# A norm and the two projections behind it, issued in a written order, and the mixer's last weights given to two token tiles first

## The chip, the cores and the metric

The kernel runs on one core of a Trainium2 chip. The metric is the device time of one execution in microseconds (us). Three executions of the kernel before took 3191.44, 3194.19 and 3197.66 us; their median is 3194.19 us.

The core has five engines with queues of their own: TensorE (PE in the profile, with its weight loads as PEld), VectorE (DVE), ScalarE (ACT), GpSimd (POOL) and SyncE (SP, which here only issues DMAs). Each executes its own queue in order; they wait for each other through semaphores.

## What is computed

A trunk of two layers over 512 tokens of 1024 elements, all in float32. A conditioning vector gives each layer a shift, a scale and a gate for each sub-layer. In each layer:

```
h = rmsnorm(x, norm_mix) * (1 + sc1) + sh1
x = x + g1 * mixer(h)      # projections of h, a gated MLP, stick-breaking attention, an output projection
h = rmsnorm(x, norm_ffn) * (1 + sc2) + sh2
x = x + g2 * peer(h)       # q = h @ wq; scores against keys; top 16 of 256; experts' u and v rows
```

and a last `rmsnorm`. So four times in the program a norm of x stands between the product that completes x and the projections that read h.

## The kernel before, in words

The 512 tokens are four tiles of 128, and the 1024 elements eight blocks k of 128. Every large product is made of three matmuls on numbers split in a high and a low part (`mm3`, lines 125 to 128): high by high, high by low, low by high. A weight block is loaded by SP's queue into `raw` (two buffers); ScalarE copies its high part into `hi`, and VectorE subtracts to get `lo` (`split`, lines 110 to 115; `weights`, lines 117 to 123). `hi` and `lo` have three buffers each, so at most three weight blocks are split at a time, and a fourth has to wait until the matmuls on the first are done. Every ninth of the PEER's query weights is subtracted on GpSimd instead (line 521).

`normed` (lines 154 to 180) makes h. It takes the tokens in two halves, tiles 2 and 3 first. GpSimd multiplies each tile's x by its reciprocal root mean square (line 166). Then, for each of four chunks of two blocks k, TensorE transposes four 128x128 pieces into PSUM (line 173), ScalarE applies scale and shift (line 176, into `tk`), and VectorE splits the result into `hh` and `hl` (lines 114 and 115). In the PEER the first half's `tk` is also transposed back (line 493), since tile 3's tokens need h with tokens on partitions (`hrow`, line 498).

Behind the norm the projections run through `ahead` (lines 130 to 136): eight blocks `w_qk` and twelve row blocks in the mixer, sixteen blocks `wq` in the PEER. Each of the first kind is 24 matmuls of 512 columns (`qk_item`, lines 274 to 283; `q_item`, lines 508 to 521), and reads h of all four tiles. The row blocks of the last group of the mixer, `vv`, are copied out of PSUM by VectorE (line 325); the attention's logits, which come next (`logits`, lines 345 to 364), use the same PSUM banks.

The mixer ends with `out_item` (lines 410 to 429): two halves of the columns, four weight blocks each, and for each block the four tiles in the order 3, 2, 0, 1. At the last block the tile's residual is added (`residual`, lines 209 to 212: two products and two sums of 128x512 for both column halves), its squares are summed on ScalarE and their root taken (`stats`, lines 148 to 152), all of which the next norm waits for. In layer 0 the modulation vectors are still being made meanwhile: `fill(n)` puts n steps into the program (`mod_steps`, lines 186 to 195), each a DMA of 512 KB and one pass of VectorE over 128x1024. The PEER ends (lines 827 to 842) with the last two weight blocks' matmuls for the tiles 2, 0 and 1 in turn, each followed by the residual and `stats`.

What sets the order: the program text gives each instruction a priority, and a scheduler at build time puts each engine's queue together, taking at every moment of its own model the earliest instruction whose inputs are ready. Under `high_priority` (lines 271 and 495) a region goes ahead of everything else. Under `manual_schedule` (line 800) the instructions of the region stay in the written order on each engine, and where they fall among the others is still the scheduler's choice. `keep_in_program_order` puts one instruction behind the one written before it on its engine: so the load of ScalarE's exponential table (line 343). Two operand-free steps of the PEER, an iota and sixteen memsets into the free part of the big array `act` (lines 551 to 554), run on GpSimd.

## Time and profile before

| | |
|---|---|
| median of three executions | 3194.19 us |
| the profiled execution's own time | 3192.75 us |
| its span | 3191.0 us |
| TensorE busy | 2993.4 us, 94% of the span |
| VectorE busy | 2505.6 us, 79% |
| ScalarE busy | 1177.2 us, 37% |
| GpSimd busy | 908.3 us, 28% |

The span is the time from the first to the last instruction on the core; the execution's time is 1.75 us more. Times in the rows are us from the start of the span, unless marked ns. A group's row gives count, busy time and mean duration of one; a bracket at the end of a timeline row gives how long the engine was idle before and what released it.

### The profile page before, as it was taken

To read this page: it belongs to the slowest core of one execution; us is meant where nothing else is said; L and a number is where in the kernel's file an instruction comes from. 1 tells how busy PE (TensorE), PEld (TensorE's weight loads), DVE (VectorE), ACT (ScalarE), POOL (GpSimd) and SP (SyncE) were. 2 spreads that over 40 slices of the span, in tenths; PEclk is the share of its full clock that TensorE was granted. 3 is DMA by queue.
4 is the path that set the end of the run, shared out by engine and by line. 5 is a ranking of instruction groups with operands and counts; after the bars stand their busy time and mean duration, and the time that the engine had idled before them with its cause. 6 is when DMAs were issued, how large, how long until landed. Compare 5 with 4: busy or idle time off the path is not lost.

```text
span 3191.0 us, 47164 instructions
## 1 busy us (share of the span) xinstructions
PE 2993.4 (94%) x17516; PEld 2633.3 (83%) x17516; DVE 2505.6 (79%) x4925; ACT 1177.2 (37%) x2016; POOL 908.3 (28%) x634
## 2 busy tenths in 40 slices
PE   6988988999999999999989989899999999999997
PEld 4776878998777999977777878889987789998776
DVE  7687799698777889777754448969887788996777
ACT  3253333333333433333333533334333334333333
POOL 1002012103555323345410010230055443333452
PEclk8989999999999999999999899999999999999999
DMA  8746223436888666688732022232388876667885
GB/s 302 251 152 212 80 73 106 133 107 240 304 302 287 246 222 234 239 322 298 276 102 86 3 99 80 93 132 100 133 297 315 303 271 230 228 240 256 308 303 203
DMA packets 178840, 651.45 MB, mean 204 GB/s; under 512 B 19850, under 2 KB 20274, under 8 KB 178610
## 3 DMA queue, kind: packets, MB, share of 16 engines
q1 hardware_dynamic: 104018, 378.14, 35.2%
q0 software_dynamic: 73728, 268.47, 22.5%
q8 instruction: 137, 2.24, 0.3%
q10 hardware_dynamic: 864, 1.84, 0.2%
q14 instruction: 93, 0.76, 0.1%
HBM read 642.08 MB, written 6.29 MB: 203 GB/s over the span
## 4 chain that ended last, share of the span: by engine, by line
PE 23%; DVE 8%; issue 7%; DMA 6%; POOL 5%; ACT 1%; POOLq 0%; DVEq 0%; ACTq 0%
PE u L126 4%; PE u L128 3%; PE u L127 3%; PE b L126 2%; PE b L128 2%; PE b L127 2%; DVE hrow L747 1%; DVE lo L115 1%; PE z L351 1%; DMA raw<-in_ut 1%; DVE act L595 1%; PE b L387 1%; PE acc L128 0%; PE acc L127 0%; PE acc L126 0%
## 5 line engine op out<-in xcount | busy, mean ns | idle before, releaser
L126 PE MATMUL u<-hh,hi 128*128 128x384 f32 x2048 | 704.6, 344 | 22.2 <-ACT act L476 19.4
L128 PE MATMUL u<-hh,lo 128*128 128x384 f32 x2048 | 690.9, 337 | 13.9 <-DVE lo L115 13.8
L127 PE MATMUL u<-hl,hi 128*128 128x384 f32 x2048 | 689.2, 337 | 0.0
L128 PE MATMUL acc<-hi,hl 128*128 128x512 f32 x1536 | 607.4, 395 | 34.6 <-DVE hl L115 34.6
L127 PE MATMUL acc<-lo,hh 128*128 128x512 f32 x1536 | 603.2, 393 | 7.1 <-DVE lo L115 6.9
L112 ACT ACTIVATE hi<-raw 128x1024 fp32r<-128x1024 f32 x368 | 388.8, 1058 | 587.7 <-PE b L127 163.1
L126 PE MATMUL acc<-hi,hh 128*128 128x512 f32 x1536 | 601.4, 392 | 0.0
L115 DVE TENSOR_TENSOR lo<-raw,hi 128x1024 fp32r<-128x1024 f32 x332 | 407.0, 1226 | 208.6 <-ACT hi L112 207.7
L126 PEld LDWEIGHTS u<-hh,hi 128*128 128x128 f32 x2048 | 387.3, 189 | 27.2 <-ACT act L476 22.3
L128 PEld LDWEIGHTS u<-hh,lo 128*128 128x128 f32 x2048 | 387.3, 189 | 17.8 <-DVE lo L115 17.7
L127 PEld LDWEIGHTS u<-hl,hi 128*128 128x128 f32 x2048 | 388.3, 190 | 0.1
L112 ACT ACTIVATE hh<-act 128x384 fp32r<-128x384 f32 x256 | 134.4, 525 | 684.4 <-PE acc L127 680.8
L128 PEld LDWEIGHTS acc<-hi,hl 128*128 128x128 f32 x1536 | 290.2, 189 | 113.5 <-DVE hl L115 54.4
L127 PEld LDWEIGHTS acc<-lo,hh 128*128 128x128 f32 x1536 | 290.1, 189 | 75.3 <-DVE lo L115 14.4
L126 PEld LDWEIGHTS acc<-hi,hh 128*128 128x128 f32 x1536 | 290.3, 189 | 58.7
L115 DVE TENSOR_TENSOR lo<-wide,hi 128x1024 fp32r<-128x1024 f32 x232 | 282.8, 1219 | 2.2 <-ACT hi L112 2.2
L112 ACT ACTIVATE hi<-wide 128x1024 fp32r<-128x1024 f32 x232 | 242.7, 1046 | 0.1
L115 POOL TENSOR_TENSOR lo<-raw,hi 128x1024 fp32r<-128x1024 f32 x36 | 93.6, 2599 | 496.4 <-ACT hi L112 478.1
L126 PE MATMUL b<-hh,hi 128*128 128x512 f32 x384 | 150.3, 395 | 20.6 <-DVE hh L114 19.2
L115 DVE TENSOR_TENSOR hl<-act,hh 128x384 fp32r<-128x384 f32 x256 | 141.2, 551 | 14.4 <-ACT hh L112 13.8
L190 DVE SCALAR_TENSOR_TENSOR aw<-aw,crow 128x1024 f32<-128x1024 f32 x96 | 119.4, 1247 | 39.6 <-DMA aw<-in_ada 39.3
L127 PE MATMUL b<-hl,hi 128*128 128x512 f32 x384 | 150.1, 392 | 0.5 <-DVE hl L115 0.5
(1505 smaller groups left out, 4995.2 us busy)
## 6 DMA issues: line engine op xcount, KB each, us to landing
raw<-in_ut SPq DMA_DIRECT2D x256, 512.0 KB
wide<-in_v_rows SPq DMA_DIRECT2D x232, 512.0 KB
aw<-in_ada SPq DMA_DIRECT2D x96, 512.0 KB
raw<-in_wq SPq DMA_DIRECT2D x32, 512.0 KB
raw<-in_w_row SPq DMA_DIRECT2D x24, 512.0 KB
raw<-in_v_rows SPq DMA_DIRECT2D x24, 512.0 KB
raw<-in_w_qk SPq DMA_DIRECT2D x16, 512.0 KB
raw<-in_w_o SPq DMA_DIRECT2D x16, 512.0 KB
```

The lines of the kernel that those rows point to most:

```text
L112: A.activation(dst_hi, src, AF.Copy)
L115: sub.tensor_tensor(dst_lo, src, dst_hi.bitcast(F32), OP.subtract)
L126: T.matmul(o, lh, rh, start=first, stop=False)
L127: T.matmul(o, lh, rl, start=False, stop=False)
L128: T.matmul(o, ll, rh, start=False, stop=last)
L190: V.scalar_tensor_tensor(aw, aw, 1.0, crow[0], op0=OP.mult, op1=OP.mult, accum_out=modc[:, l, j:j + 1])
L351: T.matmul(z[:, b], qk[rw_, 4 + p_, i * P:(i + 1) * P], qk[rw_, p_, t * P:(t + 1) * P], start=b in (0, 4), stop=False, skip_group_check=True)
L387: T.matmul(po[:, tiles.index(t)], e[:, b], vv[:, i, h * 64:(h + 1) * 64], start=i == 0, stop=i == t)
L595: V.tensor_tensor(pr[:, :w], pr[:, :w], pr[:, w:2 * w], op)
L747: V.scalar_tensor_tensor(gacc, r, wgt[:, n - P:n - P + 1], gacc, op0=OP.mult, op1=OP.add)
```

## The change

The norm is cut into functions: `scales`, `scaled` (the scaling pass, now VectorE's), `chunk` (transposes, scale and shift, split). `normed` still exists, for layer 0's first norm. The three other norms, those of both PEERs and of layer 1's mixer, are issued by `opening`, in a region whose order on each engine is as written: the first two projections' weights and accumulators are taken ahead of the norm, and their matmuls are cut in two token halves of 256 columns, so that the sums over the tiles 2 and 3 stand between the chunks of the two halves.

```
-    def normed(pool, ps, l, which, hi, lo, after=None):
+    def scaled(pool, t0):
...
+            V.tensor_scalar_mul(xn[t], held["xs"][:, t], xstat[t])
...
-                G.tensor_scalar(xn[t], held["xs"][:, t], xstat[t], 0.0, OP.mult, OP.add)
...
+    def opening(pool, ps, l, which, hi, lo, srcs, tks):
+
+        with tc.manual_schedule():
+            scs = scales(pool, l, which)
+            ws = [weights(src) for src in srcs]
+            pq = [ps.tile([P, S], F32, name="b") for _ in srcs]
+
+            def sums(t0, q):
+                ts = slice(t0 * P, (t0 + 2) * P)
+                for k in (2 * q, 2 * q + 1):
+                    sl = slice(k * P, (k + 1) * P)
+                    for (wh, wl), o in zip(ws, pq):
+                        for n, (lh, rh) in enumerate(((wh, hi), (wh, lo), (wl, hi))):
+                            T.matmul(o[:, ts], lh[:, sl], rh[:, k, ts], start=t0 == 2 and k == 0 and n == 0,
+                                     stop=t0 == 0 and k == KD - 1 and n == 2, skip_group_check=True)
+
+            xn = scaled(pool, 2)
+            for q in range(4):
+                chunk(ps, l, which, scs, xn, 2, q, hi, lo, tks(2, q))
+            xn = scaled(pool, 0)
+            for q in range(3):
+                sums(2, q)
+            chunk(ps, l, which, scs, xn, 0, 0, hi, lo, tks(0, 0))
+            sums(2, 3)
+            for q in range(1, 4):
+                chunk(ps, l, which, scs, xn, 0, q, hi, lo, tks(0, q))
+            for q in range(4):
+                sums(0, q)
+        return pq
```

In the mixer, layer 1 uses it; the copy of `vv` out of PSUM goes to ScalarE; and the last three weight blocks of `w_o` are all taken before their matmuls, which go through the tiles 3 and 2 first and then through 0 and 1:

```
+                if l == 0:
+                    with tc.high_priority():
+                        normed(nm, ps, l, 0, hh, hl)
+                    opened = []
+                else:
+                    opened = opening(nm, ps, l, 0, hh, hl, [w_qk[l, j] for j in range(OPEN)],
+                                     lambda t0, q: nm.tile([P, 2, 2 * P], F32, name="tk", bufs=2))
...
-                ahead([qk_item(j) for j in range(8)]
+                for j, pq in enumerate(opened):
+                    qk_done(j, pq)
+                ahead([qk_item(j) for j in range(len(opened), 8)]
...
-                      + row_items(w_row[l, 2], lambda t, pr: V.tensor_copy(vv[:, t], pr)))
+                      + row_items(w_row[l, 2], lambda t, pr: A.activation(vv[:, t], pr, AF.Copy)))
...
-                ahead([out_item(half, kk) for half in range(2) for kk in range(4)])
+                ahead([out_item(0, kk) for kk in range(4)] + [out_item(1, 0)])
+                ended = [out_item(1, kk)[0]() for kk in range(1, 4)]
+                for tiles in (ORDER[:2], ORDER[2:]):
+                    for kk in range(1, 4):
+                        out_item(1, kk, tiles)[1](ended[kk - 1])
                 fill(96)
```

In the PEER the scaled tokens of the first half are kept in the free part of `act`, and the transposes back come after the opening; the iota is kept behind what is written before it on GpSimd. `qk_done` and `q_done` are the ends of the old items, split off.

```
-                    with tc.high_priority():
-                        normed(nm, ps, l, 1, hh, hl, back)
-                    for half, ph in enumerate(kept):
+
+                    free = act[0][:, :12].rearrange("p b t -> p (b t)")
+                    tks = [free[:, n * 512:(n + 1) * 512].rearrange("p (a t) -> p a t", a=2) for n in range(6)]
+                    opened = opening(nm, ps, l, 1, hh, hl, [wq[l, j] for j in range(OPEN)],
+                                     lambda t0, q: tks[q] if t0 else tks[4 + q % 2])
+                    for half in range(2):
+                        ph = ps.tile([P, 512], F32, name="b")
+                        for k in range(4 * half, 4 * half + 4):
+                            T.transpose(ph[:, k % 4 * P:(k % 4 + 1) * P], tks[k // 2][:, k % 2, P:], ident)
                         A.activation(hrow[:, half * 512:(half + 1) * 512], ph, AF.Copy)
...
-                    ahead([q_item(j) for j in range(16)])
+                    for j, pq in enumerate(opened):
+                        q_done(j, pq)
+                    ahead([q_item(j) for j in range(len(opened), 16)])
...
-                    G.iota(jk, pattern=[[1, 16], [0, P]], base=0, channel_multiplier=0,
+                    first_ = G.iota(jk, pattern=[[1, 16], [0, P]], base=0, channel_multiplier=0,
                            allow_small_or_imprecise_dtypes=True)
+                    tc.keep_in_program_order(first_)
```

## Rows read from the trace of the kernel before

**Rows 1.** The page's busy times: us (share of the span) xinstructions

```profile
PE 2993.4 (94%) x17516; PEld 2633.3 (83%) x17516; DVE 2505.6 (79%) x4925; ACT 1177.2 (37%) x2016; POOL 908.3 (28%) x634
```

**Rows 2.** TensorE's timeline, three norms: start us, us, work [idle <-releaser]

```profile
298.78 0.39 PE L128 MATMUL b<-hi,hl 128*128 128x512 f32 x1
320.34 0.94 PE L126 MATMUL b<-hh,hi 128*128 128x512 f32 x3 [0.69 <-PE b L173]
...
1614.32 0.39 PE L128 MATMUL acc<-hi,hl 128*128 128x512 f32 x1
1629.61 1.02 PE L126 MATMUL b<-hh,hi 128*128 128x512 f32 x3
...
1870.21 0.39 PE L127 MATMUL b<-lo,hh 128*128 128x512 f32 x1
...
1873.16 0.39 PE L128 MATMUL b<-hi,hl 128*128 128x512 f32 x1
...
1890.57 0.94 PE L126 MATMUL b<-hh,hi 128*128 128x512 f32 x3 [0.69 <-PE b L173]
```

**Rows 3.** Timeline of TensorE, layer 0, where the attention logits begin

```profile
166.56 2.50 PE L351 MATMUL z<-qk 64*128 64x128 f32 x10 [7.49 <-DVE uvw L325]
```

**Rows 4.** Line 325, both layers: who waited for it (us, times)

```profile
  PE z L351: 8.3, 2
```

**Rows 5.** Timeline of ScalarE, a projection's result copied out of PSUM

```profile
1636.63 0.58 ACT L281 ACTIVATE qk<-b 128x512 f32<-128x512 f32 x1
```

**Rows 6.** Tile tk, durations of one in ns (min/median/max)

```profile
L176 ACT ACTIVATE tk<-b,modc,sc x64: 554/564/581, 21.5 to 1892.8; 128x256 f32<-128x256 f32 x64
L114 DVE CAST hh<-tk x48: 409/422/1220, 23.3 to 1893.4; 128x512 fp32r<-128x512 f32 x48
L115 DVE TENSOR_TENSOR hl<-tk,hh x48: 678/691/1481, 24.8 to 1893.9; 128x512 fp32r<-128x512 f32 x48
...
L212 DVE TENSOR_TENSOR xs<-xs,tk x16: 680/683/1997, 276.1 to 1875.6; 128x512 f32<-128x512 f32 x16
```

**Rows 7.** Tile xn, durations of one in ns (min/median/max)

```profile
L166 POOL TENSOR_SCALAR xn<-xs,rs x16: 1114/1394/2622, 9.8 to 1887.0; 128x1024 f32<-128x1024 f32 x16
```

**Rows 8.** The page's costliest groups: the two passes over a loaded weight block

```profile
L112 ACT ACTIVATE hi<-raw 128x1024 fp32r<-128x1024 f32 x368 | 388.8, 1058 | 587.7 <-PE b L127 163.1
...
L115 DVE TENSOR_TENSOR lo<-raw,hi 128x1024 fp32r<-128x1024 f32 x332 | 407.0, 1226 | 208.6 <-ACT hi L112 207.7
```

**Rows 9.** Timeline of VectorE, four one-input passes of 512 elements

```profile
1830.06 1.68 DVE L240 TENSOR_SCALAR y<-y,rsy 128x512 f32<-128x512 f32 x4 [1.12 <-POOL rsy L141]
```

**Rows 10.** Windows, layer 1's PEER norm: each engine's busy time, PEclk, DMA share, GB/s

```profile
1875.00:1878.00 3.00, 0.00 (x0) 0.00 (x0) 2.63 (x6) 2.77 (x5) 2.81 (x2) 0.59 1.02 416
1878.00:1882.00 4.00, 2.29 (x9) 1.60 (x10) 0.51 (x2) 1.02 (x2) 4.00 (x5) 0.50 0.84 338
1882.00:1886.00 4.00, 3.73 (x15) 2.58 (x14) 3.07 (x6) 2.60 (x6) 3.56 (x17) 0.52 0.02 6
1886.00:1890.00 4.00, 2.62 (x18) 1.96 (x18) 1.98 (x3) 2.45 (x6) 2.44 (x3) 1.00 0.00 0
```

**Rows 11.** TensorE's timeline, attention of layer 1: 256-column matmuls among others

```profile
1779.89 0.28 PE L377 MATMUL z<-sh,tri 128*128 128x256 f32 x1
1780.01 0.40 PE L376 MATMUL z<-sl,tri 128*128 128x512 f32 x1
...
1781.39 0.60 PE L373 MATMUL z<-sh,tri 128*128 128x256 f32 x3
```

**Rows 12.** Timeline of GpSimd in layer 1's PEER norm

```profile
1879.95 1.94 POOL L551 IOTA act<- 128x2048 f16 x1
```

**Rows 13.** Timeline of VectorE, a modulation step beside GpSimd's work, layer 0

```profile
295.30 3.08 DVE L190 SCALAR_TENSOR_TENSOR aw<-aw,crow 128x1024 f32<-128x1024 f32 x1 [1.16 <-DMA aw<-in_ada]
```

**Rows 14.** Timeline of TensorE, the first projection of the program

```profile
40.54 1.19 PE L126 MATMUL b<-hh,hi 128*128 128x512 f32 x2 [19.21 <-DVE hh L114]
```

**Rows 15.** VectorE's timeline, the program's start: a modulation step and its wait

```profile
18.50 1.23 DVE L190 SCALAR_TENSOR_TENSOR aw<-aw,crow 128x1024 f32<-128x1024 f32 x1 [0.96 <-DMA aw<-in_ada]
```

More of the change, by code (lines that the diff above doesn't have):

```diff
@@ L51 @@
 LOOK = 2
+OPEN = 2
 QM = 9
@@ L152, in stats, with scales @@
         rsqrt_mean(xstat[t], ss, D, 1)
-    def normed(pool, ps, l, which, hi, lo, after=None):
+    def scales(pool, l, which):
         m = modc[:, l]
@@ L160, in normed, with chunk @@
                                    col(l, which)[:, 2 * q:2 * q + 2], op0=OP.add, op1=OP.mult)
-        sh = m[:, 24 * which:24 * which + 8]
+        return scs
+    def scaled(pool, t0):
+        xn = {}
+        for t in (t0, t0 + 1):
+            xn[t] = pool.tile([P, D], F32, name="xn", bufs=2)
+            V.tensor_scalar_mul(xn[t], held["xs"][:, t], xstat[t])
+        return xn
+    def chunk(ps, l, which, scs, xn, t0, q, hi, lo, tk):
+        sh = modc[:, l, 24 * which:24 * which + 8]
+        pt = ps.tile([P, 2, 2 * P], F32, name="b")
+        for kk in range(2):
+            k = 2 * q + kk
+            for t in (t0, t0 + 1):
+                T.transpose(pt[:, kk, (t - t0) * P:(t - t0 + 1) * P], xn[t][:, k * P:(k + 1) * P], ident)
+        for kk in range(2):
+            k = 2 * q + kk
+            A.activation(tk[:, kk], pt[:, kk], AF.Identity, scale=scs[q][:, kk:kk + 1], bias=sh[:, k:k + 1])
+        both = slice(t0 * P, (t0 + 2) * P)
+        split(hi[:, 2 * q:2 * q + 2, both], lo[:, 2 * q:2 * q + 2, both], tk, V)
@@ L162, in normed @@
+    def normed(pool, ps, l, which, hi, lo):
+        scs = scales(pool, l, which)
         for t0 in (2, 0):
-            xn = {}
-            for t in (t0, t0 + 1):
-                xn[t] = pool.tile([P, D], F32, name="xn", bufs=2)
-                G.tensor_scalar(xn[t], held["xs"][:, t], xstat[t], 0.0, OP.mult, OP.add)
+            xn = scaled(pool, t0)
             for q in range(KD // 2):
-                pt = ps.tile([P, 2, 2 * P], F32, name="b")
-                tk = pool.tile([P, 2, 2 * P], F32, name="tk", bufs=2)
-                for kk in range(2):
-                    k = 2 * q + kk
-                    for t in (t0, t0 + 1):
-                        T.transpose(pt[:, kk, (t - t0) * P:(t - t0 + 1) * P], xn[t][:, k * P:(k + 1) * P], ident)
-                for kk in range(2):
-                    k = 2 * q + kk
-                    A.activation(tk[:, kk], pt[:, kk], AF.Identity, scale=scs[q][:, kk:kk + 1], bias=sh[:, k:k + 1])
-                both = slice(t0 * P, (t0 + 2) * P)
-                split(hi[:, 2 * q:2 * q + 2, both], lo[:, 2 * q:2 * q + 2, both], tk, V)
-                if after is not None and t0 == 2:
-                    after(q, tk[:, :, P:])
+                chunk(ps, l, which, scs, xn, t0, q, hi, lo, pool.tile([P, 2, 2 * P], F32, name="tk", bufs=2))
@@ L408, in mixer, with out_item @@
                 po = {}
-                def out_item(half, kk):
+                def out_item(half, kk, tiles=ORDER):
                     def use(w):
                         wh, wl = [a.rearrange("p (a b) -> p a b", a=2) for a in w]
-                        for t in ORDER:
+                        for t in tiles:
                             if kk == 0:
@@ L485, in peer @@
                 with tc.tile_pool(name="nm", bufs=1) as nm:
-                    kept = []
-                    def back(q, src):
-                        if q % 2 == 0:
-                            kept.append(ps.tile([P, 512], F32, name="b"))
-                        for kk in range(2):
-                            o = (q % 2 * 2 + kk) * P
-                            T.transpose(kept[-1][:, o:o + P], src[:, kk], ident)
-                    with tc.high_priority():
-                        normed(nm, ps, l, 1, hh, hl, back)
-                    for half, ph in enumerate(kept):
+                    free = act[0][:, :12].rearrange("p b t -> p (b t)")
[6 more added lines that the diff above has]
+                            T.transpose(ph[:, k % 4 * P:(k % 4 + 1) * P], tks[k // 2][:, k % 2, P:], ident)
                         A.activation(hrow[:, half * 512:(half + 1) * 512], ph, AF.Copy)
@@ L514, in use, with q_done @@
                             mm3(pq, wh[:, sl], wl[:, sl], hh[:, k], hl[:, k], k == 0, k == KD - 1)
-                        qts[j] = qp.tile([P, S], F32, name="qt", bufs=4)
-                        A.activation(qts[j], pq, AF.Copy)
-                        if ranked:
-                            best(*ranked.pop(0))
-                        if j % 4 == 3:
-                            ranked.extend((t, j - 3, score(t, j - 3)) for t in order)
-                    return lambda: weights(wq[l, j], G if j % QM == 1 else V), use
+                        q_done(j, pq)
+                    return lambda: weights(wq[l, j], G if j % QM == 1 else V), use
+                def q_done(j, pq):
+                    qts[j] = qp.tile([P, S], F32, name="qt", bufs=4)
+                    A.activation(qts[j], pq, AF.Copy)
+                    if ranked:
+                        best(*ranked.pop(0))
+                    if j % 4 == 3:
+                        ranked.extend((t, j - 3, score(t, j - 3)) for t in order)
                 ranked = []
```

9 lines of the change are left out of this document (6 added, 3 removed).

## The prediction

> **What bounds the kernel now.** TensorE is busy in 94% of the span [rows 1], so time can come from TensorE's work or from its roughly 190 us of idling; the change adds and removes almost no work, so I looked for the idling at the places it touches. The timeline of TensorE shows three holes in dense work, one at each norm that gets the new order. The dense work before them ends at the last row's start plus its 0.39 us, and the next projection's matmuls start at the first row with `hh` in it [rows 2]: 299.17 to 320.34 (PEER, layer 0), 1614.71 to 1629.61 (mixer, layer 1) and 1873.55 to 1890.57 (PEER, layer 1). The holes are 21.2, 14.9 and 17.0 us, 53.1 together. Only transposes run in them. A fourth hole is at the logits of layer 0, where TensorE waits 7.49 us for VectorE's copies of `vv` [rows 3].
>
> **What the openings are worth.** The unit is the dense matmul of 512 columns: between the rows at 1870.21 and 1873.16 there are 13 steps in 2.95 us, 0.227 us each [rows 2]. The first two projections, 48 matmuls, took 10.9 us behind each hole. Now they run inside it, as 96 matmuls of 256 columns. A 256-column one, with its own weight load, starts 0.12 us before the next matmul [rows 11]: 11.5 us in all, 1.44 us for each `sums` of twelve.
>
> I work out layer 1's PEER in us from E, the end of the mixer's last matmul.
> - Two tiles first: the second half of the last three blocks is 2 x 3 x 6 matmuls, 8.2 us, so tile 2 is complete at E-8.2 and tile 3 at E-9.5; by the old order it was E-2.7 and E-4.1. Their residuals (two passes of 0.68 us each [rows 6]) and roots are done well before E.
> - Weights: three blocks are split at a time, so the second projection's block can be split only when the middle one of the last three is done, E-2.7. ScalarE's pass of 1.06 and VectorE's of 1.23 [rows 8] put it at E-0.4. It is written ahead of the scaling passes, so these wait for it too. The third of the last `w_o` blocks must wait for the block before the three, E-16.3, and is ready at E-14 against a need at E-10.9; I cost that at nothing, with 3 us of cover.
> - VectorE then has residuals 0 and 1 (1.36 each, the second not before E) to E+2.3, and two scaling passes. Such a pass isn't in the trace on VectorE; bounds are 0.42 for 512 elements [rows 9] and GpSimd's 1.39 for 1024 [rows 7]. I take twice the first, 0.84, the nearest kind. E+4.0.
> - First chunk: four transposes at the low clock, 15 in 3.73 us [rows 10], 1.0; ScalarE twice 0.56, VectorE 0.42 and 0.69 [rows 6]. E+7.2; three more chunks at VectorE's 1.1 each, E+10.5. Then the second half's scaling, E+12.2; by then three `sums` are done (the third can't start before E+9.4).
> - Second half: transposes 0.6 (18 in 2.62 us at full clock [rows 10]), ScalarE 1.1, four chunks on VectorE to E+18.3, the last `sums` to E+19.8. The other `sums` lie beside this. The eight transposes back, once inside the hole, now follow: 1.2 us, E+21.0.
>
> Take off the 10.9 us that the two projections cost anyway, and the hole is 10.1 us instead of 17.0: **6.9 us** gained. In layer 0's PEER the same 10.1 stand against 21.2: **11.1**. There the old hole was longer because GpSimd had iota and memsets ahead of the second half's scaling (the same row in layer 1 [rows 12]) and VectorE had modulation steps. In layer 1's mixer the residual of the last tile is four passes, 2.7, and both final weight blocks are held to E, so the second block's split follows E too: 2.7 + 1.2 + 1.7 puts the first transposes at E+5.6 instead of E+4.0; no transposes back. 10.5 against 14.9: **4.4**.
>
> **What comes off that.** The clock: 1.3 us after E it had fallen to the lower of its levels in part, stayed at 0.50 to 0.52 (1.2 GHz) through 8 us in which only transposes ran, and was back at 1.00 (2.4 GHz) in the stretch after [rows 10]. In the new order TensorE also idles after E, so the first `sums` meet the low clock. At double spacing two of them cost 2.9 us more, of which 1.3 lie before E+12.2: 1.5 an opening, **-4.5**. Bounds are 0 and all 96 matmuls (a rival below). Layer 0's modulation steps: the last nine now stand before the tiles 3 and 2 are complete, at twice the density; a pass is 1.2 us, up to 3.08 beside GpSimd [rows 13, 15]. Bounds 0 and nine passes, 11 us; they started E-16 and end near E, so I take **-1.5**. The query block that GpSimd split goes to VectorE, before E, hidden. Layer 0's first norm has its four scaling passes on VectorE, whose splits TensorE waits for there [rows 14]: bounds +1 (no port shared with GpSimd) and -3.4; VectorE also waits for DMAs between its steps, 0.96 us in one [rows 15], so **-0.5**.
>
> **The copies of `vv`.** ScalarE does the same copy in 0.58 [rows 5], right behind each tile's last matmul: the logits can begin some 0.6 us plus a release after 159.07 instead of 7.49. **+6.3**; bounds 0 (ScalarE is late: the table load is now written behind the copies) and 6.9. What follows, the gating and the attention, keeps its own pace and moves forward. Of the 8.3 us in both layers [rows 4], 0.8 are layer 1's, where a copy of the same length still ends the wait: nothing. The iota, kept behind earlier GpSimd work, is needed only behind sixteen projections of over 5 us each: nothing.
>
> **Sum.** 6.9 + 11.1 + 4.4 - 4.5 - 1.5 - 0.5 + 6.3 = 22.2 us. The profiled execution took 3192.75 us, 1.44 under the median of 3194.19; the sum makes it 3170.6, and on the median's footing **3172 us**. Behind the openings TensorE sets the pace until the gathers, which hang on the steps and not on absolute times, so I let the gain stand to the end.
>
> **A rule against it.** The two matmuls 0.12 us apart [rows 11] show a weight load hidden behind a 256-column stream. The Trainium skill, "TensorE: Matmul & The Clock Gate", section "The mechanism", says that a weight load overlaps with a matmul in flight only if it targets another row group; here every load fills all rows. By that, with the page's 107 ns for a load and some 109 for the stream, each of the 96 would cost 0.216 us, some 9 us more an opening, and the sum would be some 5 us slower than before; the rows contradict it, and what is left of it is the first rival.
>
> **The rivals.**
> - *Loads show at 256 columns.* Three 256-column matmuls in a group took 0.60 us where one takes 0.28: 0.16 apart [rows 11]. Then 96 x 0.04 = 3.8 us an opening: 22.2 - 11.5 = 10.7, 3183.5 us. For: twelve in a row, with alternating weights. Against: the 0.12. 10%.
> - *The order holds only within the region.* Other work is put between its steps, the third projection's block above all (1.06 on ScalarE, 1.23 on VectorE [rows 8]): 2.3 us an opening, 6.9 in all, 3179 us. For: where the region's steps fall among others is the scheduler's choice. Against: both engines have pauses that could take it. In this way the change wouldn't do quite what it says. 10%.
> - *Only the copies pay.* The strict order makes VectorE a chain with waits of its own (weight splits, the squares of tile 1, modulation steps) and the openings end where the old ones did: -5.8 us, 3188. 12%.
> - *Slower: the clock stays low through the openings.* Place: from E to the last `sums`. Price: 32 transposes at 0.25 and 96 matmuls at 0.24 are 31 us. From E+4.0, with 2 us of transposes back and less the 10.9, that is 26.1 against 21.2 and 17.0; in the mixer 25.7 against 14.9: 24.8 lost, 5.8 kept by copies and start, 3213 us. It decides when some 74 of the 96 run at half rate (26.7 us over three openings, at 0.12 each). For: openings are a patchwork of short bursts. Against: the clock was back while only transposes ran, with gaps [rows 10]. 7%.
>
> **How the numbers follow.** My forecast has 61%, with a range of its own of 3158 to 3182. A measurement of this kernel can tell 0.2%, 6.4 us, from no change. Faster by more: the forecast, the first two rivals, and a little of the third, 0.83. Within: most of the third, 0.09. Slower: the clock, and a bit for a late block in the mixer, 0.08. The range that holds eight of ten reaches from 3156 (no clock loss, no modulation loss, shorter scaling) to the third rival, 3188.
>
> **What would show it.** TensorE's timeline: the hole before the first `sums` about 7 us in the PEERs and 8.5 in the mixer, matmuls of 256 columns 0.12 us apart, the last `sums` some 20 us after E; logits of layer 0 at about 160. VectorE the busiest engine from E to the last chunk. I am wrong if the 256-column steps are 0.16 or more, if the granted clock stays at 0.5 past the third `sums`, if E itself comes later after its stage's start, or if VectorE stands idle behind a weight split while x is ready.

## The result, and the profile after

The changed kernel took 3162.37 us (median of 4 runs, 3155.86 to 3168.14) against 3192.82 us for the kernel before, run beside it (4 runs, 3184.29 to 3197.66): a ratio of 0.9905, interval 0.9887 to 0.9923, 30 us. The forecast was 3172 us, the range 3156 to 3188. The profiled execution took 3168.14 us with a span of 3166.4, so the two traces differ by 24.6 us, of which the prediction's sum is 22.2. That the two agree is partly luck, as the stages show. Below each stage runs from the start of one row to the start of another, in both traces: the first logits row of TensorE, the last `values` row, the last dense matmul of a mixer or of the layer's V stage (called E; the prediction counts from its end, 0.39 us later), ScalarE's last query copy.

| stage | before | after | difference | forecast |
|---|---|---|---|---|
| start to first logits, layer 0 | 166.6 | 159.1 | -7.5 | -5.8 |
| first logits to E, layer 0 | 132.2 | 141.3 | **+9.0** | 0 |
| E to last query copy, layer 0 | 123.6 | 119.3 | **-4.3** | -8.1 |
| that to E of the V stage, layer 0 | 1192.0 | 1187.9 | -4.1 | 0 |
| E to first logits, layer 1 | 125.2 | 123.1 | -2.1 | -2.9 |
| first logits to last values, layer 1 | 86.6 | 76.5 | **-10.0** | 0 |
| last values to E, layer 1 | 47.1 | 47.1 | 0 | 0 |
| E to last query copy, layer 1 | 119.4 | 113.6 | -5.8 | -5.4 |
| that to the end | 1198.4 | 1198.6 | +0.2 | 0 |

By its last query copy layer 0 had gained 2.7 us where the forecast had 13.9, 11 us too little; layer 1's attention gave 10 us that were not forecast at all. TensorE's share of the span is what it was [rows 1]:

```profile
PE 2985.8 (94%) x17660; PEld 2639.4 (83%) x17660; DVE 2503.4 (79%) x4935; ACT 1179.8 (37%) x2024; POOL 878.8 (28%) x616
```

Layer 1's PEER is the opening as it was meant. TensorE's timeline of the kernel after answers to [rows 2]; the columns are the same:

```profile
1854.23 0.39 PE L129 MATMUL b<-hi,hl 128*128 128x512 f32 x1
1857.51 0.45 PE L178 MATMUL b<-ident,xn 128*128 128x128 f32 x1 [2.89 <-DVE ms L141]
1858.19 3.46 PE L178 MATMUL b<-ident,xn 128*128 128x128 f32 x15 [0.23 <-DVE xn L168]
1861.30 0.56 PE L205 MATMUL b<-hh,hi 128*128 128x256 f32 x1
1861.66 0.41 PE L205 MATMUL b<-hl,hi 128*128 128x256 f32 x1
1861.87 0.41 PE L205 MATMUL b<-hh,lo 128*128 128x256 f32 x1
...
1863.91 0.28 PE L205 MATMUL b<-hh,hi 128*128 128x256 f32 x1
1864.03 0.28 PE L205 MATMUL b<-hl,hi 128*128 128x256 f32 x1
...
1866.78 0.60 PE L178 MATMUL b<-ident,xn 128*128 128x128 f32 x4
...
1875.73 0.28 PE L205 MATMUL b<-hh,lo 128*128 128x256 f32 x1
1875.85 1.04 PE L548 MATMUL b<-ident,act 128*128 128x128 f32 x8
1876.65 0.47 PE L127 MATMUL b<-hh,hi 128*128 128x512 f32 x1
```

The dense work ends at 1854.62 (1854.23 + 0.39). The first sums start 6.7 us behind that, the last one 21.1, the next projection 22.0. The matmuls of 256 columns are 0.21 apart until about 1863.9 and 0.12 apart then. The granted clock in the windows of the same stretch (columns as in [rows 10]) says why:

```profile
1858.00:1862.00 4.00, 3.81 (x18) 3.82 (x19) 3.00 (x7) 3.12 (x9) 3.56 (x18) 0.50 0.84 315
1862.00:1866.00 4.00, 4.00 (x29) 4.00 (x28) 3.93 (x7) 0.96 (x3) 0.00 (x0) 0.78 0.04 12
1866.00:1870.00 4.00, 4.00 (x37) 4.00 (x37) 1.14 (x3) 1.72 (x4) 0.00 (x0) 1.00 0.00 0
```

Layer 0's PEER is not. TensorE, the kernel after:

```profile
300.38 0.39 PE L129 MATMUL b<-hi,hl 128*128 128x512 f32 x1
310.10 4.03 PE L178 MATMUL b<-ident,xn 128*128 128x128 f32 x16 [9.33 <-DVE xn L168]
...
313.78 0.52 PE L205 MATMUL b<-hh,hi 128*128 128x256 f32 x1
...
327.46 0.28 PE L205 MATMUL b<-hh,lo 128*128 128x256 f32 x1
```

The first sums start 13.0 us behind the last matmul's end instead of 6.7. VectorE's timeline of the stretch between shows what it did first:

```profile
300.45 1.22 DVE L230 SCALAR_TENSOR_TENSOR aw<-aw,crow 128x1024 f32<-128x1024 f32 x1
...
303.87 1.23 DVE L230 SCALAR_TENSOR_TENSOR aw<-aw,crow 128x1024 f32<-128x1024 f32 x1 [0.85 <-DMA aw<-in_ada]
...
305.02 1.29 DVE L251 TENSOR_TENSOR tk<-b,grow 128x512 f32<-128x512 f32 x2
306.77 1.23 DVE L230 SCALAR_TENSOR_TENSOR aw<-aw,crow 128x1024 f32<-128x1024 f32 x1 [0.46 <-DMA aw<-in_ada]
...
309.20 1.41 DVE L168 TENSOR_SCALAR xn<-xs,rs 128x1024 f32<-128x1024 f32 x2
```

Three modulation steps (`aw`, line 230) stand at E and behind it, among the last residuals, two of them with a wait for their row. The scaling passes come behind the third.

The copies of `vv` did what they were to do to the logits [rows 3], and TensorE lost it again 11 us later:

```profile
158.04 0.39 PE L129 MATMUL b<-hi,hl 128*128 128x512 f32 x1
159.11 1.38 PE L401 MATMUL z<-qk 64*128 64x128 f32 x10 [0.69 <-ACT uvw L375]
...
170.28 2.07 PE L384 MATMUL b<-uvw,ws 128*128 128x256 f32 x4 [7.57 <-DVE y L385]
```

VectorE's timeline has the cause of that wait, again modulation steps, ahead of the gating (`y`, line 385) in its order:

```profile
157.68 1.23 DVE L230 SCALAR_TENSOR_TENSOR aw<-aw,crow 128x1024 f32<-128x1024 f32 x1 [1.52 <-DMA aw<-in_ada]
...
163.90 1.22 DVE L230 SCALAR_TENSOR_TENSOR aw<-aw,crow 128x1024 f32<-128x1024 f32 x1 [2.51 <-DMA aw<-in_ada]
...
165.60 1.23 DVE L230 SCALAR_TENSOR_TENSOR aw<-aw,crow 128x1024 f32<-128x1024 f32 x1 [0.47 <-DMA aw<-in_ada]
...
168.59 1.23 DVE L230 SCALAR_TENSOR_TENSOR aw<-aw,crow 128x1024 f32<-128x1024 f32 x1 [1.69 <-DMA aw<-in_ada]
...
169.75 0.87 DVE L385 SCALAR_TENSOR_TENSOR y<-b,cols,uvw 128x256 f32<-128x256 f32 x2
```

Last, the 10 us of layer 1's attention. Windows of the kernel before (columns as above, the clock is the third from the right):

```profile
1739.00:1755.00 16.00, 14.86 (x81) 10.83 (x81) 11.51 (x21) 11.02 (x20) 1.01 (x1) 1.00 0.10 33
1755.00:1765.00 10.00, 9.57 (x38) 7.14 (x39) 5.81 (x12) 4.42 (x7) 0.00 (x0) 0.55 0.01 2
1765.00:1776.00 11.00, 11.00 (x49) 10.27 (x49) 4.34 (x7) 4.58 (x9) 0.00 (x0) 0.50 0.00 0
```

and of the kernel after, at the same work:

```profile
1746.00:1757.00 11.00, 10.75 (x76) 8.69 (x75) 8.41 (x16) 7.63 (x14) 0.06 (x1) 1.00 0.01 1
1757.00:1767.00 10.00, 10.00 (x80) 9.25 (x78) 5.68 (x9) 6.91 (x13) 0.00 (x0) 1.00 0.00 0
```

Before, TensorE was busy throughout but stood at the lower level (0.50, 1.2 GHz) for some 20 us; after, the same stretch ran at 1.00 (2.4 GHz). The change has no edit in that stage but the copies ahead of it.

### The profile page after: what moved, and what is told of

The parts are those of the page before. It is cut to its first block, busy times and chain, and to the rows that moved or that the text cites. A ratio compares the mean times of both kernels' runs of the same rounds, so it can differ in the third digit from the quotient of the medians.

```text
span 3166.4 us, 47439 instructions
## 1 busy us (share of the span) xinstructions
PE 2985.8 (94%) x17660; PEld 2639.4 (83%) x17660; DVE 2503.4 (79%) x4935; ACT 1179.8 (37%) x2024; POOL 878.8 (28%) x616
## 4 chain that ended last, share of the span: by engine, by line
PE 48%; DVE 16%; DMA 13%; issue 11%; POOL 9%; ACT 1%; POOLq 0%; DVEq 0%; ACTq 0%
PE u L127 9%; PE u L129 8%; PE u L128 8%; DMA aw<-in_ada 3%; PE b L127 3%; PE b L129 3%; PE b L128 3%; DVE hrow L804 2%; DVE lo L116 2%; PE acc L129 2%; PE acc L128 2%; PE acc L127 2%; PE z L401 1%; DVE act L652 1%; DVE aw L230 1%
## 5 line engine op out<-in xcount | busy, mean ns | idle before, releaser
L127 PEld LDWEIGHTS u<-hh,hi 128*128 128x128 f32 x2048 | 388.9, 190 | 24.6 <-ACT act L530 19.6
L116 DVE TENSOR_TENSOR hl<-act,hh 128x384 fp32r<-128x384 f32 (+1 forms) x272 | 152.8, 562 | 14.5 <-ACT hh L113 13.6
L127 PE MATMUL b<-hh,hi 128*128 128x512 f32 x336 | 132.2, 394 | 20.7 <-DVE hh L115 20.7
L527 ACT ACTIVATE gu<-u 128x384 f32<-128x384 f32 (+23 forms) x186 | 63.8, 343 | 203.7 <-PE u L129 203.7
```

Of the source, the lines that this page charges most:

```text
L116: sub.tensor_tensor(dst_lo, src, dst_hi.bitcast(F32), OP.subtract)
L127: T.matmul(o, lh, rh, start=first, stop=False)
L527: A.activation(g[:, :n], pu[:, :n], AF.Gelu_apprx_tanh)
```

## Experiments

Each kernel was timed against the kernel before on one chip. Executions of one kernel scatter (21 of the kernel before, on one chip, from 3181.3 to 3203.5), and chips differ a little (its median lay between 3189.2 and 3199.1), so across chips the ratios are compared. The stages of each kernel's one profiled execution, taken as in the table above:

| kernel | median, us | ratio, interval | first logits L0 | E, L0 | E to last query, L0 | E to logits, L1 | attention L1 | E to last query, L1 |
|---|---|---|---|---|---|---|---|---|
| before | 3192.8 | 1 | 166.6 | 298.8 | 123.6 | 125.2 | 86.6 | 119.4 |
| after | 3162.4 | 0.9905, 0.9887-0.9923 | 159.1 | 300.4 | 119.3 | 123.1 | 76.5 | 113.6 |
| vv_back | 3173.1 | 0.9945, 0.9926-0.9965 | 167.2 | 299.1 | 117.8 | 123.2 | 77.3 | 112.8 |
| vv_only | 3183.5 | 0.9976, 0.9961-0.9991 | 158.2 | 295.9 | 123.7 | 126.4 | 76.5 | 119.7 |
| wo_back | 3168.4 | 0.9933, 0.9914-0.9952 | 159.2 | 296.6 | 120.4 | 123.1 | 76.5 | 113.9 |
| aw_deep | 3160.0 | 0.9909, 0.9892-0.9927 | 153.9 | 295.8 | 118.0 | 123.1 | 76.5 | 112.9 |
| vv_l0_back | 3169.6 | 0.9917, 0.9897-0.9938 | 166.0 | 297.9 | 117.9 | 123.1 | 76.5 | 112.9 |
| vv_l1_back | 3165.6 | 0.9907, 0.9885-0.9929 | 160.9 | 300.3 | 118.8 | 123.2 | 77.3 | 113.0 |
| no_openings | 3180.0 | 0.9947, 0.9929-0.9965 | 157.4 | 298.4 | 125.5 | 126.6 | 76.5 | 118.2 |
| xn_gp | 3165.9 | 0.9904, 0.9880-0.9927 | 159.2 | 295.3 | 121.8 | 122.1 | 76.5 | 113.7 |
| late | 3166.7 | 0.9925, 0.9901-0.9950 | 162.7 | 296.8 | 113.0 | 130.2 | 76.5 | 113.1 |
| late_vv_back | 3179.7 | 0.9960, 0.9941-0.9979 | 165.3 | 301.6 | 112.9 | 133.4 | 84.6 | 112.9 |
| late_before | 3194.0 | 1.0007, 0.9987-1.0027 | 165.2 | 296.4 | 120.1 | 130.7 | 77.3 | 119.8 |
| late_light | 3158.7 | 0.9890, 0.9861-0.9920 | 158.6 | 299.2 | 113.0 | 133.8 | 76.5 | 112.9 |

What is left, the U and V stages, holds the same work in all of them and still took 1184.7 to 1195.4 us in layer 0 and 1195.2 to 1210.3 in layer 1. A single profiled end time therefore says little; the stages that the edits touch repeat within a us or so in layer 1 where the clock stays up, and within some 5 us in layer 0.

**The copies of `vv`, both layers** (vv_back, and vv_only on the kernel before with the opposite edit):

```
-  row_items(w_row[l, 2], lambda t, pr: A.activation(vv[:, t], pr, AF.Copy))
+  row_items(w_row[l, 2], lambda t, pr: V.tensor_copy(vv[:, t], pr))
```

> The kernel after the change with one edit undone: the copies of vv go back to VectorE, in both layers. Theory (waits for modulation rows): in layer 0 the earlier logits buy nothing, because VectorE, which takes its instructions in order, stands before the modulation rows and TensorE then waits for VectorE's gating; in layer 1 the same edit is what kept TensorE's clock at full level through the attention. Then layer 0 costs 0 to 2 us more, layer 1's attention 10 us more, with the granted clock at 0.50 to 0.55 for some 20 us of it: 3162.4 + 11 = 3173 us. Rival 1 (the edit is worth what the prediction said, in layer 0, and nothing in layer 1): 3162.4 + 6.3 = 3169 us, first logits of layer 0 at about 166.5, layer 1's attention at clock 1.00. Rival 2 (the edit is worth nothing anywhere; the fall of the clock in layer 1 had another cause): 3162 us, both attentions as in the kernel after.

> The kernel before with one edit alone: the copies of vv on ScalarE, in both layers. Theory: layer 0's logits start some 7 us earlier but the end of layer 0's attention moves by under 2 us; in layer 1 the clock stays at 1.00 through the attention and its end comes some 10 us earlier: 3192.8 - 10 = 3183 us. Rival 1 (layer 0 pays, layer 1 doesn't): 3186.5 us. Rival 2 (nothing anywhere): 3193 us, with the granted clock of layer 1's attention again near 0.5 for some 20 us.

By the ratios the copies are worth 12.8 us in the kernel after (0.9945 against 0.9905; with both intervals taken together some 4 to 21) and 7.7 in the kernel before (2.9 to 12.4). But the mechanism that I had written down for layer 1 was not in vv_back's profile: its attention there took 77.3 us at clock 1.00. So that fall of the clock isn't tied to the edit in every execution, and the edit had to be split by layer.

**By layer** (vv_l0_back, vv_l1_back: the same line with `if l == 0`, `if l == 1`):

> The kernel after with the copies of vv back on VectorE in layer 0 alone. The two runs on this edit as a whole put it at about 10 us by the medians (3173.1 without it, 3183.5 with it alone), and their profiles show only some 2 to 4 us of it at the end of layer 0's mixer. Theory (the worth is layer 1's: there the copy on VectorE leaves TensorE a patch of short waits in which the granted clock can fall, 10 us when it does): 3162 to 3165 us, layer 1's attention from first logits to last values 76.5 us. Rival 1 (the worth is layer 0's earlier logits, 6.3 us and more, as predicted): 3169 to 3173 us. Rival 2 (both layers half): 3167 us.

> The kernel after with the copies of vv back on VectorE in layer 1 alone. Theory (the worth is layer 1's): 3168 to 3173 us, with executions some 10 us apart, since in one profile with that copy on VectorE the clock fell in layer 1's attention (86.6 us) and in another it didn't (77.3 us). Rival 1 (layer 0's): 3162 us, layer 1's attention at 76.5 to 77.5 us and clock 1.00. Rival 2 (both half): 3167 us.

The intervals overlap, so the times don't tell the layers apart. The profiles say more when taken together. Layer 0: the first logits come at 166.0 to 167.2 with the copies on VectorE (before, vv_back, vv_l0_back) and at 157.4 to 160.9 with them on ScalarE (after, vv_only, wo_back, vv_l1_back, no_openings, xn_gp). The E behind them is at 298.6 on average in the one group (297.9 to 299.1) and at 297.8 in the other (295.3 to 300.4). Of 7.6 us at the logits 0.8 are left at E, and with a scatter of 5 us in the second group the 0.8 can't be told from nothing. Part of that scatter is a second fall of the granted clock in layer 0's attention (last section): the three profiles of this group that have it put E at 298.4 to 300.4, the three without it at 295.3 to 296.6, which is 2.7 us ahead of the first group. Layer 1: without a fall of the clock the copy on VectorE costs 0.8 us in the attention (77.3 against 76.5). With it, the clock fell there in 2 profiles of 5 (before, late_vv_back: 86.6 and 84.6 us), without it in none of 9. The falls cost 9.3 and 7.3 us over the 77.3. That makes 0.8 + 0.8 + 2/5 of 8.3 = 5 us on average, inside the intervals of both comparisons, but near their lower ends: where the rest of the 8 to 13 us comes from is not shown. If the fall were as frequent with either copy, two falls in 14 profiles would both land among these five in 11% of cases; so that it is more frequent with the copy on VectorE is suggested and not settled.

**The last projection** (wo_back: all four tiles by each block, as before):

```
-  ahead([out_item(0, kk) for kk in range(4)] + [out_item(1, 0)])
-  ...
+  ahead([out_item(half, kk) for half in range(2) for kk in range(4)])
```

> The kernel after with the mixer's last projection in its old order: all four token tiles by each of the eight weight blocks. Theory: the openings need tiles 3 and 2 early. Without that, VectorE has the residuals of all four tiles to do behind the last matmuls (tile 2 complete 2.7 us before the end instead of 8.2), some 4 passes of 0.68 us more after the end: the first sums of layer 1's PEER come 2 to 3 us later after the last matmul, two PEER openings: 3162.4 + 5 = 3167 us. Rival (VectorE's chain of residuals was done in its pauses anyhow, and the earlier second weight block makes up for it): 3160 to 3163 us, the first sums within 1 us of 6.7 behind the last matmul in layer 1.

By time 0.9933 against 0.9905 is 9 us, with both intervals some 1 to 17. The stages show 1.4 of it: 1.1 in layer 0's query stage and 0.3 in layer 1's. In layer 1's PEER the first transposes start 3.7 us behind the last matmul's start instead of 3.3 and the first sums 7.4 instead of 7.1: the rival is nearer, two tiles first is worth well under a us there. What the order is worth to the whole kernel stays open between the times and the stages.

**More buffers for the modulation rows** (aw_deep):

```
+  deep[:] = nm, 8
...
+  deep[:] = at, 4
...
+  deep[:] = rg, 4
...
-  fill = (lambda n: mod_steps(mx, n)) if l == 0 else (lambda n: None)
+  fill = (lambda n: mod_steps(deep[0], n, deep[1])) if l == 0 else (lambda n: None)
```

> The kernel after with more buffers for the modulation rows in layer 0's mixer: the eight that its start already has serve the projections too, four in the attention, four in the last projection, instead of two throughout. Nothing else is changed. Theory: with two buffers a row's transfer (4.3 us to landing) can't start before the pass two rows earlier, so VectorE waits for rows (44.6 us over the program) and holds up the gating of layer 0 and the residuals ahead of layer 0's PEER. With them gone, layer 0's gating follows the logits without the wait of 7.6 us, and the first sums of layer 0's PEER come some 4 us earlier behind the last matmul: 3162.4 - 10 = 3152 us, waits for these rows under 15 us. Rival 1 (the transfers are limited by bandwidth or by their queue, so deeper buffers move the wait and not the end): 3160 to 3164 us, waits for rows still over 35 us. Rival 2 (more rows in flight delay the weight blocks on the same queue): 3165 to 3172 us, with TensorE waiting for the blocks' splits in layer 0's projections.

The waits for rows fell to a third, the time stayed within the interval: the time of rival 1, without its reason. The waits views, kernel after and then this one (us in total, times, longest):

```profile
DVE aw L230 <- DMA aw<-in_ada: 44.6, 41, 2.7
```

```profile
DVE aw L230 <- DMA aw<-in_ada: 15.0, 19, 1.9
```

The first logits come 5.2 us earlier, but TensorE's wait for the gating is still there, 6.68 us instead of 7.57 (TensorE's timeline of this run):

```profile
164.61 2.07 PE L388 MATMUL b<-uvw,ws 128*128 128x256 f32 x4 [6.68 <-DVE y L389]
```

VectorE runs seven steps of 1.23 us between 153.22 and the gating at 164.08, none of them with a wait of over 0.67 us. The last values come at 242.9 instead of 253.3; then the last projection takes 52.9 us instead of 47.1, and E is 4.6 us earlier. In that stage VectorE is idle for under 2 us from 248 on, and TensorE waits 3.96 us for a split: the steps' own time counts there, not only their waits. So the loss is VectorE's load, and better supply moves it on.

**The openings together** (no_openings: the kernel before with the copies and the order of the last projection), and **the scaling passes alone** (xn_gp):

```
-  V.tensor_scalar_mul(xn[t], held["xs"][:, t], xstat[t])
+  G.tensor_scalar(xn[t], held["xs"][:, t], xstat[t], 0.0, OP.mult, OP.add)
```

> The kernel before with the copies of vv on ScalarE and the mixer's last projection two tiles first, but none of the three openings (norms as before, scaling passes on GpSimd, transposes back inside). Theory (the three openings are worth 4 to 6 us each in the PEERs and 2 in the mixer, and the order of the last projection pays only through them): 3183.5 us, as with the copies alone, within 3 us; the hole behind the last matmul of each mixer as in [rows 2]. Rival 1 (two tiles first pays by itself, since the old norm starts with the same two tiles): 3175 to 3179 us, the first transposes 2 to 4 us earlier behind the last matmul. Rival 2 (the openings are worth little, and the rest is the order and the copies): 3166 to 3172 us.

> The kernel after with the norm's scaling passes back on GpSimd, in the openings and in layer 0's first norm; everything else of the openings stays. A pass is 1.39 us there [rows 7] against 0.75 on VectorE (measured after). Theory (the strict order makes these passes serial with the chunks, so their place counts): first sums 1.4 us later behind the last matmul in layer 1's PEER (2 x 0.64); the second half's passes run beside VectorE's chunks instead of among them and give back about 1.4: 3162.4 + 0 to 3 = 3162 to 3165 us. Rival (GpSimd's own work, iota and memsets, comes ahead of the second half again, as it did before in layer 0): layer 0's PEER 6 to 8 us longer from the last matmul to the end of the query stage: 3169 us.

0.9947 against 0.9905 makes the openings 13.4 us (0.0042 of 3193; with both intervals some 5 to 22). The profiles put 6.3 + 3.5 + 4.5 = 14.3 us between the two at the three norms. Rival 1 of no_openings holds in part: ahead of the old norm, two tiles first brings the first transposes of layer 1's PEER 2.7 us forward (2.2 us behind the last matmul, 4.9 in vv_only) and its query stage 1.5, while layer 0's query stage is 1.8 longer. By the ratios (0.9947 and 0.9976) the order is worth 9 us here, with both intervals some 2 to 17, as it was in wo_back; the stages don't account for it here either. So the whole gain of 30 us divides, by times, into 8 for the copies, 9 for the order of the last projection and 13 for the openings. Where the scaling passes run matters little: layer 0's PEER 2.5 us longer on GpSimd, layer 1's mixer 1.0 shorter, layer 1's PEER the same, though its first sums come 0.8 us earlier on GpSimd and not 1.4 later, and no difference in time.

**Taking the steps away from layer 0** (late; late_before is the kernel before with the same edit, late_vv_back also has the copies on VectorE):

```
-  fill = (lambda n: mod_steps(mx, n)) if l == 0 else (lambda n: None)
+  plan = dict(qk=2, row=2, att=1, out=0) if l == 0 else dict(qk=1, row=2, att=0, out=0)
+  fill = lambda n: mod_steps(mx, plan[n])
...
+  if l == 1:
+      crow[0] = spread_rows(mx.tile([P, D], F32, name="crow"), ps, "b", crow[1])
...
-  if n < NU:
+  if n < NU and n % 2 == 0:
...
-  fill(96)
```

> The kernel after with 32 of layer 1's 48 modulation steps moved out of layer 0's mixer into layer 1's own (one at each query and key block, two at each row block of its projections); layer 0's attention keeps every second step and its last projection has none. The row that the steps multiply by is built again in layer 1 (eight transposes, two copies). Nothing is left out. Theory (VectorE's steps eat the gain of layer 0: 16 of them in the attention, 24 in the last projection and up to the opening): layer 0's attention takes 77 to 82 us from first logits to last values instead of 94.2, its E comes some 12 us earlier, and PEER's opening there takes what it takes in layer 1 (113.6 us from E to the last query eviction instead of 119.3); layer 1 pays 2 to 3 us for the row and the steps: 3162.4 - 12 - 5.6 + 2.5 = 3147 us. Rival 1 (it was the clock alone, after whatever wait, and not the steps): layer 0's attention still 89 to 94 us, 3160 us. Rival 2 (the steps only move: in layer 1 they delay the splits of its projections, which the opening's gain hangs on): layer 1's projections 10 us longer, 3160 us.

> The same kernel with fewer steps in layer 0, and the copies of vv back on VectorE in both layers. Theory (with the steps out of the way the earlier logits of layer 0 stand to the end of its mixer): E of layer 0 comes 6 to 8 us later than in the run without this edit, 3147 + 7 = 3154 us. Rival (the gain of the copies is lost in the attention even so, by the clock): E within 3 us, 3147 to 3150 us.

> The kernel before with the same move of 32 modulation steps into layer 1, and nothing of the change. Theory: the old order gains less from it than the new one. Layer 0's attention 77 to 80 us instead of 85.2, its PEER's opening some 4 us shorter, layer 1 2.5 us longer: 3193 - 6 - 4 + 2.5 = 3185 us, so that the change is worth 38 us where the steps are out of its way. Rival (the steps cost both kernels the same): 3193 - 15 = 3178 us, the change worth about 31 us as it is now.

The opening of layer 0's PEER becomes that of layer 1: 113.0 us from E to the last query copy instead of 119.3, and the first transposes start as they do there. TensorE's timeline of this run:

```profile
296.79 0.39 PE L129 MATMUL b<-hi,hl 128*128 128x512 f32 x1
300.07 0.30 PE L178 MATMUL b<-ident,xn 128*128 128x128 f32 x1 [2.89 <-DVE ms L141]
```

3.3 us from row to row where the kernel after has 9.7. So the steps cost that opening 6.3 us (4.8 to 7.4 by the other profiles with the opening as it is and the steps in layer 0, 117.8 to 120.4); with them gone the new order is 7.1 us better than the old one (113.0 against 120.1). Layer 0's attention gained less than expected: 87.0 us from first logits to last values against 94.2, not 77 to 82, with the granted clock again low for part of it. And layer 1 paid 7.1 us more up to its logits, not 2.5: both rivals hold in part, and the time came out no better (0.9925). In the kernel before the move bought nothing at all, against both numbers expected: layer 0 gained 5.8 us up to its last query copy, and layer 1 lost 5.4 up to its logits. The two runs with the copies differ by 13 us in the median, their E by 4.8, and this profile of late_vv_back has the fall of the clock in both attentions: the question of the copies stays where it was, with a third comparison of times (0.9960 against 0.9925, 11 us) above what the profiles account for.

**The same, lighter on layer 1** (late_light: `qk=0, row=2, out=1` in layer 1, and the row kept in memory):

```
-  plan = dict(qk=2, row=2, att=1, out=0) if l == 0 else dict(qk=1, row=2, att=0, out=0)
+  plan = dict(qk=2, row=2, att=1, out=0) if l == 0 else dict(qk=0, row=2, att=0, out=1)
...
+  nc.scalar.dma_start(out=crow[0], in_=crowd)
```

> The kernel after with the same 32 steps moved, but lighter on layer 1: none at its query and key blocks, two at each row block of its projections and one at each of the first eight blocks of its last projection; the row that they multiply by goes out to memory in layer 0 and comes back by a DMA instead of being built again. In the run before this one layer 0 ended its query stage 9.9 us earlier than the kernel after, and layer 1 gave back 7.1 us between E and its logits (steps' transfers ahead of the opening's weights, the row's transposes, one wait of 2.9 us for a split). Theory (that price was the place of the steps, not the steps): layer 0 as there, E to the logits of layer 1 123 to 126 us, 3162.4 - 9.9 + 2 = 3155 us. Rival 1 (any step in layer 1's projections costs what it saved in layer 0): E to logits 130 us again, 3162 to 3167 us. Rival 2 (steps at the last projection of layer 1 hold up its PEER's opening as they did in layer 0): E to the last query eviction of layer 1 116 to 119 us instead of 113.6, 3159 us.

By its place rival 1: 133.8 us from E to the logits, worse than in the run before it; rival 2 not, with 112.9 us from E to the last query copy. VectorE's timeline shows what stood in the way, in the middle of the opening of layer 1's mixer:

```profile
1609.18 1.23 DVE L231 SCALAR_TENSOR_TENSOR aw<-aw,crow 128x1024 f32<-128x1024 f32 x1
...
1614.96 1.22 DVE L231 SCALAR_TENSOR_TENSOR aw<-aw,crow 128x1024 f32<-128x1024 f32 x1
...
1617.04 1.22 DVE L231 SCALAR_TENSOR_TENSOR aw<-aw,crow 128x1024 f32<-128x1024 f32 x1
```

Eight such steps stand there in all until VectorE's last chunk; the last `sums` start 32.2 us behind E's end where the kernel after has 23.8. How the 10.7 us between the two stages divide is not shown: the granted clock was also at the lower level for 13.7 us here against 6.8, and TensorE later waits 2.2 us for a split. These steps stand behind the row blocks in the program, which come after six more query and key blocks. They depend only on their rows, so the scheduler put them between VectorE's chunks, inside the region whose order is given by hand. The median is 3.7 us under that of the kernel after, measured apart, and the intervals of the ratios (0.9890 and 0.9905) overlap: no version here is shown to beat the changed kernel.

## Why the prediction came out as it did

- **Layer 1's PEER: right.** Forecast 6.9 less 1.5 of clock, 5.4; measured 5.8. Of the ledger, first sums E+7.2 against 6.7, the next projection E+21.0, 22.5 with the clock, against 22.0. One step came at its time for another reason: the second half's transposes, at E+12.2, waited for the three `sums` written ahead of them and not for VectorE, whose scaling was done at E+11.4. VectorE, which was to be the busiest engine, was then busy for 1.14 us of 4 (1866 to 1870). The scaling pass that the trace of before didn't show took 0.75 us where I had 0.84. Two tiles first, which the ledger begins with, counts for little in these stages (wo_back), whatever the times say of it.
- **Layer 1's mixer: right**, 2.9 against 2.1; first transposes E+5.6 against 5.4 (1613.26 behind 1607.89). A third block's split did fall between two chunks (1.22 us at 1618.01), as the rival "the order holds only within the region" had it, at about half the 2.3 us that it named:

```profile
1618.01 1.22 DVE L116 TENSOR_TENSOR lo<-raw,hi 128x1024 fp32r<-128x1024 f32 x1
```

- **256 columns: right.** The step is 0.12 us at the upper level and 0.21 at the lower one. The Trainium skill, "TensorE: Matmul & The Clock Gate", section "The mechanism", says in its list that a load overlaps only with a matmul on another row group; the 96 matmuls here, each with a full-row load, contradict that as the prediction applied it. A sentence earlier in the same section also lets a load for the background weight buffer go ahead of matmuls in flight, which the prediction left out; whether that is what happens here no row shows.
- **The clock: right in kind, too large in size.** The first dozen sums of layer 1's PEER ran at the lower level, 12 x 0.09 = 1.1 us, against the 1.5 forecast. In layer 1's mixer it was the first four or five, some 0.5 us, and in layer 0's PEER one or two, 0.25: 1.9 us in all, not 4.5. Before the change, the clock fell near 2 us behind E (0.59 is the mean of 3 us [rows 10]), not 1.3.
- **Layer 0's PEER: mis-sized**, 8.1 against 4.3. The step that failed is "they started E-16 and end near E, so I take -1.5": the steps cost 6.3 us (after against late), inside the bounds of 0 to 11. Without them the stage gained 10.6 us (123.6 to 113.0) where the forecast without that term has 9.6. The last three run at E and behind it, between the residuals that the opening waits for. I had counted the steps as VectorE time before E and not asked what was queued behind them.
- **The copies: the step that failed outright** is "What follows, the gating and the attention, keeps its own pace and moves forward". It doesn't in layer 0: 7.6 us at the logits are 0.8 at E on average. The gating runs on VectorE behind modulation steps that wait for rows, TensorE then waits 7.57 us, and the granted clock is low for part of the attention after that. So the long wait at the logits only moved on to the gating; aw_deep shows that it stays, at 6.68 us, when the steps hardly wait for rows any more. It is one of the prediction's own signs of being wrong: E came 9.0 us later after the first logits.
- **Layer 1's attention: not foreseen.** "0.8 are layer 1's ... nothing" left out the clock. The wait at the logits is still there, as it said (0.69 us after, 0.8 before), and the attention itself is 0.8 us shorter; the rest of the 10 us of the profiled pair came from a fall of the granted clock, which 2 of 5 profiles with the copies on VectorE have. Why it falls stays open.
- **Layer 0's first norm: no difference**, where 0.5 was taken off. With the scaling passes back on GpSimd (xn_gp) the first logits come at 159.2 against 159.1.

So the sum of 22.2 was near the 24.6 of the traces because 11 us too many in layer 0 met 10 us of clock and 4 us of scatter in layer 0's U and V stages. The openings, forecast at 16.4 together, gave 12.2 in the two traces and 14.3 against the profile of no_openings, so that half of the prediction is of the size that the stages show. By the ratios they gave 13.4 without the order of the last projection, which the forecast counts in them, and 22.7 with it. Within it two errors met: the clock was taken some 2.6 us too high and layer 0's steps 4.8 too low.

## What to carry to other kernels

Removing a wait of TensorE gains only as much as the next engine in the chain can keep up with. Before counting on it, look at what stands ahead of the next consumer in that engine's order, and whether those instructions wait for transfers. Filler work without dependencies goes wherever the scheduler finds a place, also into a region that was ordered by hand, so its place has to be fixed too, and its engine time counted where it lands. Where executions scatter by 20 us, compare stages between fixed rows of several profiles, not end times of two. Where times and stages disagree, as over the order of the last projection here, leave the question open.

## What the chip showed that was not expected

The same instructions in the same order, in two kernels that differ only behind that point (after and wo_back), took 94.2 and 88.7 us for layer 0's attention. TensorE's wait for the gating makes 1.8 us of that (7.57 and 5.78); the rest goes with the granted clock, in windows of the kernel after and of wo_back (us, TensorE's busy time, clock, DMA share, GB/s):

```profile
189.00:199.00 10.00, 9.21 (x57) 0.78 0.31 104
199.00:209.00 10.00, 9.56 (x66) 0.88 0.35 109
```

```profile
189.00:199.00 10.00, 8.98 (x71) 1.00 0.34 113
199.00:209.00 10.00, 9.56 (x73) 1.00 0.58 202
```

In both, TensorE had waited for VectorE before and had been at the lower level (0.50 and 0.58 in the window from 169 to 179). In one it fell a second time though TensorE was busy for 8.8 us of 10 in the window before and 9.2 in the one shown; over the 50 us from 159 on the windows' means make 20 us at the lower level in one and 10 in the other. Five of the 14 profiles have this second fall in layer 0's attention (after, vv_l1_back, no_openings, late_light, late_vv_back). What decides it no run here shows. The Trainium skill, "TensorE: Matmul & The Clock Gate", section "What's actually happening", says that the number of matmuls at the lower level varies between runs of one kernel. It says so of the kernel's start; the two profiles here, of kernels alike up to this point, show such a difference in the middle.
